# A fp32 decoder block on one core: the gate/up products of the FFN with the weight tiles stationary and h^T moving

## The chip, the cores and the metric

The kernel runs on one core of one Trainium2 chip. The metric is device time in microseconds (us) of one execution. Three runs of the kernel before took 446.09, 446.21 and 446.27 us; the median is 446.21 us.

## The reference, cut to what matters

A decoder block over 256 tokens of width 1024, all in float32: two branches (a causal convolution of 31 taps with layer norm, and attention over 8 heads), gated and merged, then a SwiGLU feed-forward with d_ff = 2816.

```python
n = rmsnorm(x, norm1_g);  z = n @ w_in                 # 1024 x 7168
cu, cg, q, k, v, gc, ga = split(z)
merged = sigmoid(gc) * conformer_conv(cu, cg) + sigmoid(ga) * (attention(q, k, v) @ w_attn_out)
h = x + merged @ w_out
h = h + (silu(r @ w_gate) * (r @ w_up)) @ w_down       # r = rmsnorm(h, norm2_g), d_ff = 2816
```

## The kernel before, in words

Every product is made of three products of float32r parts: the left operand is split in a high and a low part (h^T in `hh` and `hl`), the weights in `whi` and `wlo`, and high x high, low x high and high x low are summed in PSUM (`mm3`, lines 141 to 143).

The work is a list of 146 slots. A slot is one piece of weights: 512 KB, two k-tiles of 128 rows by 512 columns. In a slot TensorE does 12 matmuls: for each of 2 token tiles and 2 k-tiles the three products. The stationary operand is a 128x128 tile of the left side (tokens as columns), the moving operand 512 columns of weights, and the sum is 128 tokens x 512 columns. So each matmul loads its own stationary tile and then streams 512 columns. The slots of the gate/up product are `gu0` to `gu10` (44 slots; a chunk holds 256 gate columns and the same 256 up columns), those of the down product `dn0`, `dn1` (22 slots).

The order is written out by hand. `stream_dma` issues weights from SP 11 slots ahead into 5 buffers `raw`; `stream_split` has ScalarE make `whi` (line 123) and VectorE or GpSimd make `wlo` (line 124) 6 slots ahead. Other work hangs on the slots in four lists: `pre` (ahead of the slot's matmuls), `jobs` (between the two token tiles), `post` (after them) and `late`. All engines run their own instructions in the order in which they were written.

At the start, `stream_dma` puts on SP, in turn: piece 0 part 0, `xt` tile 0, piece 0 part 1, `xt` tile 1, `xt` tiles 2 and 3, piece 1, and so on (`between`, `load_x`, line 605). ScalarE scales and rounds x (`xgh`, line 617), squares it (lines 627, 630), GpSimd adds the squares (lines 631, 633), and `first_norm`, after slot 4, has TensorE sum them over partitions (`ss`, line 648). `WARM` = 8 matmuls of zeros keep TensorE busy from the start (line 161).

After the last slot of the out projection (`out_done`), h is transposed by TensorE (`htr`, line 513, one half of its 8 k-tiles per column block), split into `hh` and `hl` (lines 518, 519), and its row sums of squares give `rstd2` (lines 525 to 528). Since tokens lie on the partitions of the sums, `rstd2` is a per-partition scalar. For each chunk, `ffn_done` computes silu(gate) on ScalarE (line 546), multiplies on VectorE (line 548), has TensorE transpose the result (`ftr`, line 560: 4 transposes of 128x128), and splits it into `fh` and `fl` (lines 561, 562), the stationary side of the down product.

Where tiles lie: SBUF tiles follow each other in the order of their pools, each rounded up to 32 bytes a partition. `raw`, `whi`, `wlo` (4096 bytes each) and the pairs in `t8` (`xg`, `ao`, `y`, `m`, `h`; 8192 bytes each) all start at the same place modulo 512 bytes. `fh` and `fl` start behind the pool `sm`. Its tiles other than `bst` (192 bytes), `mv`, `lr`, `s2` (32 each), and `sq`, `m`, `nmx`, `den` (two of 32 each) are multiples of 512 bytes: 192 + 3 x 32 + 8 x 32 = 544, so `fh` and `fl` lie 32 bytes past the place of the weights modulo 512.

At the end the last three slots of the second half of the down product are done per token tile, the last one in two halves of 256 columns (`end`, 36 matmuls of 256 columns), and `store` adds the residual (line 571).

Of the kernel before, what the change touches and what calls it, by code (L numbers as in the profile page):

```python
# [27 lines left out]
EPS = 1e-6  # L28
BIG = 1e30
# [22 lines left out]
WARM = 8  # L52
# [3 lines left out]
class Chunk:  # L56
    """CW output columns of one product, for all tokens: nk k-tiles in pieces of G."""

    def __init__(self, name, w, lhs, nk, done):
        self.name, self.w, self.lhs, self.nk, self.done = name, w, lhs, nk, done  # L60
        self.acc = None


@with_exitstack
def hybrid_block(ctx: ExitStack, tc: tile.TileContext, x, xT, par, w_in, w_co, w_ao, w_o, w_gu, w_dn, out):
# [20 lines left out]
    def add(*chunks):  # L86
        """One chunk, or two of which each half is done in turn."""
        n = chunks[0].nk // G
# [7 lines left out]

    def parts(i):
        return [slice(j, j + 1) for j in range(G)] if i < 3 else [slice(0, G)]

    def stream_dma(upto):  # L100
        while at["dma"] < min(upto, len(slots)):
            i = at["dma"]
            c, g = slots[i]
            raw[i] = wp.tile([P, G, CW], F32, tag="raw", bufs=RAW_BUFS, name=f"raw{i}")
# [8 lines left out]
    def stream_split(upto):  # L113
        while at["split"] < min(upto, len(slots)):
            i = at["split"]
            hi[i] = wp.tile([P, G, CW], F32R, tag="whi", bufs=SPL_BUFS, name=f"whi{i}")
            lo[i] = wp.tile([P, G, CW], F32R, tag="wlo", bufs=SPL_BUFS, name=f"wlo{i}")
# [14 lines left out]

    def mm3(c, i, g, t, acc=None, cols=slice(0, CW), first=0, last=None):
        """Piece g of the chunk for token tile t; the sum runs from k-tile first to last."""
        xh, xl = c.lhs()
        acc = c.acc[t] if acc is None else acc
        last = c.nk - 1 if last is None else last
        tok = slice(t * P, (t + 1) * P)
        for j in range(G):
            k = g * G + j  # L140
            nc.tensor.matmul(acc, xh[:, k, tok], hi[i][:, j, cols], start=(k == first), stop=False)  # L141
            nc.tensor.matmul(acc, xl[:, k, tok], hi[i][:, j, cols], start=False, stop=False)  # L142
            nc.tensor.matmul(acc, xh[:, k, tok], lo[i][:, j, cols], start=False, stop=(k == last))  # L143

# [1 line left out]
    prm = cst.tile([P, N_PAR], F32, name="prm")  # L146
    xt = ea.tile([P, KD, S + 1], F32, tag="vs", name="xt")
    xs = cst.tile([P, T, D], F32, name="xs")

# [1 line left out]
    warm = cst.tile([P, CW], BF16, name="warm")  # L151
# [6 lines left out]
    load_table(AF.Sigmoid)  # L158
    wps = bank("wps", CW)
    for _ in range(WARM):  # L160
        nc.tensor.matmul(wps, warm[:, :P], warm, start=True, stop=True)
    ident = cst.tile([P, P], F32, name="ident")
    make_identity(nc, ident)
    mhalf = cst.tile([P, 8], F32, name="mhalf")
# [40 lines left out]
    def refill(ch):  # L205
        """The channels of the next tile go on the partitions, after KC - 1 zeros."""
# [17 lines left out]
    def run_taps(slot, until):  # L224
        while load["dve"] + TAP <= until:
# [94 lines left out]
    def normed(name, b):  # L320
        def done(slot, acc):
            st = {}

            def squares(t):
# [3 lines left out]
                for h in range(4):  # L328
                    junk = sm.tile([P, P], F32, tag="junk", name="junk")
# [37 lines left out]
    def head(first, slot, h):  # L367
# [15 lines left out]
        def score():  # L383
            s["bias"] = sm.tile([P, 3, P], F32, tag="bias", name=f"bias{h}")
            nc.scalar.mul(s["bias"], dist, 2.0 ** (-8.0 * (h + 1) / H))
            s["sc"] = bank(f"sc{h}", 4, P)
            nc.tensor.matmul(s["sc"][:, 0, :], s["q"][:, :P], s["k"][:, :P], start=True, stop=True)
            nc.tensor.matmul(s["sc"][:, 1:3, :], s["q"][:, P:], s["k"], start=True, stop=True)
# [106 lines left out]
    s2 = sm.tile([P, T, 2], F32, bufs=1, name="s2")  # L495

    def out_done(b):
        cols = slice(b * CW, (b + 1) * CW)

        def done(slot, acc):  # L500
# [4 lines left out]
            def turn():  # L505
                if not hT:
                    hT[0] = pair("h")
# [14 lines left out]
            def squares():  # L522
# [3 lines left out]
                if b:  # L526
# [9 lines left out]
    ff = {}  # L536

    def ffn_done(c):
        def done(slot, acc):
            f = {}  # L540

            def gate():
                for t in range(T):
                    r = rstd2[:, t : t + 1]
                    sg = sm.tile([P, 256], F32, tag="e0", name=f"fs{c}{t}")
                    nc.scalar.activation(sg, acc[t][:, :256], AF.Silu, scale=r)  # L546
                    f[t] = sm.tile([P, 256], F32, tag="e1", name=f"f{c}{t}")
                    nc.vector.scalar_tensor_tensor(f[t], acc[t][:, 256:], r, sg, op0=ALU.mult, op1=ALU.mult)  # L548

            def turn():  # L550
                if not ff:
                    early.close()
                    late_pool = ctx.enter_context(tc.tile_pool(name="ff", bufs=1))
                    ff[0] = (late_pool.tile([P, KF, S], F32R, name="fh"), late_pool.tile([P, KF, S], F32R, name="fl"))
                fh, fl = ff[0]
                k2 = slice(2 * c, 2 * c + 2)
                tr = bank(f"ftr{c}", 2, S)
                for j in range(2):
                    for t in range(T):
                        nc.tensor.transpose(tr[:, j, t * P : (t + 1) * P], f[t][:, j * P : (j + 1) * P], ident)  # L560
                nc.scalar.copy(fh[:, k2, :], tr)  # L561
                nc.vector.tensor_sub(fl[:, k2, :], tr, fh[:, k2, :].bitcast(F32))

            pre[slot + 1].append(gate)
            jobs[slot + 2].append(turn)
        return done
# [27 lines left out]
    ffn = [Chunk(f"gu{c}", w_gu[c], lambda: hT[0], KD, ffn_done(c)) for c in range(FF // 256)]  # L594
    add(*ffn[:2])
    for c in ffn[2:]:
        add(c)
# [4 lines left out]
    xg[0] = pair("xg")  # L602

    def load_x(k0, k1):
        nc.sync.dma_start(xt[:, k0:k1, :], xT[:, k0:k1, :])

    def between(i, part):
        if i == 0:
            load_x(part.start, part.stop)
# [5 lines left out]
    def split_x(k):  # L615
        g = xt[:, k, S:]
        nc.scalar.activation(xg[0][0][:, k, :], xt[:, k, :S], AF.Copy, scale=g)
        nc.vector.scalar_tensor_tensor(xg[0][1][:, k, :], xt[:, k, :S], g, xg[0][0][:, k, :].bitcast(F32),
                                       op0=ALU.mult, op1=ALU.subtract)

    stream_dma(AHEAD)
    sq = ea.tile([P, 2, S], F32, tag="yt", name="sq0")

    def square(q):
        """Squares of x, summed over the parts of its rows that share a partition."""
        if q == 0:
            nc.scalar.activation(sq, xt[:, :2, :S], AF.Square)
            return
        s = sm.tile([P, 2, S], F32, tag="u", name=f"xsq{q}")
        nc.scalar.activation(s, xt[:, 2 * q : 2 * q + 2, :S], AF.Square)  # L630
# [11 lines left out]
    ones = cst.tile([P, 1], F32, name="ones")  # L642
    nc.gpsimd.memset(ones, 1.0)

# [18 lines left out]
    for slot, (c, g) in enumerate(slots):  # L663
        for job in pre.pop(slot, ()):
            job()
        if g == 0:
            c.acc = [ps.tile([P, CW], F32, tag="mm", bufs=4, name=f"{c.name}_{t}") for t in range(T)]
        if slot < n - tail:
# [5 lines left out]
        if slot < n - tail:  # L674
            mm3(c, slot, g, 1, last=split_k - 1 if c is slots[-1][0] else None)
            if slot == n - tail - 1:
                nc.vector.tensor_add(xs[:, 1, D - CW :], xs[:, 1, D - CW :], c.acc[1])
# [17 lines left out]
        if g == c.nk // G - 1:  # L695
# [50 lines left out]
```

## Time and profile before

| | |
|---|---|
| time, median of 3 runs | 446.21 us (446.09 to 446.27) |
| span of the profiled execution | 443.5 us (its own time is not listed apart; the median less the span is 2.7 us) |
| TensorE matmuls (PE) | busy 437.6 us, 99% of the span, 2026 records |
| weight loads (PEld) | busy 359.6 us, 81% |
| VectorE (DVE) | 309.6 us, 70% |
| ScalarE (ACT) | 243.9 us, 55% |
| GpSimd (POOL) | 87.5 us, 20% |
| gate/up stage | 252.6 to 377.7 us of the span |

PE records are pipelined: a matmul of 512 columns shows 390 ns, but the next one starts some 230 ns after it. What counts is the distance between starts, called the pitch here. A product of plain float32 operands shows as two records. The weight load of a matmul stands in a row of its own (PEld) and overlaps the matmul ahead of it.

### The profile page before, as it was taken

The numbers are of one execution on the slowest core, as the hardware profiler recorded it, in microseconds if no ns is written. First come the engines' busy times: TensorE is split into PE (matmuls) and PEld (weight loads), VectorE is DVE, ScalarE is ACT, GpSimd is POOL, SyncE is SP. The second block draws the span as 40 slices with busy tenths as digits, with TensorE's granted clock in tenths as the row PEclk, the third lists the DMA queues.
The fourth block names the chain that finished last, engine by engine and source line by source line (L and its number), as shares of the span: only waits on it lengthen the run. The fifth ranks groups of instructions, "written<-read, shape, count | busy, mean of one in ns | idle before, by whom it ended". The sixth has DMA issues, their size and how long they took to land.

```text
span 443.5 us, 5743 instructions
## 1 busy us (share of the span) xinstructions
PE 437.6 (99%) x2026; PEld 359.6 (81%) x2026; DVE 309.6 (70%) x523; ACT 243.9 (55%) x439; POOL 87.5 (20%) x73
## 2 busy tenths in 40 slices
PE   8999999999999999999999999999999999999997
PEld 4788888888888888888888888888888888888886
DVE  5989999898899799967586575555555555644501
ACT  6854466689998676639325374444444444633200
POOL 1614465745462443100000000000000000000000
PEclk9999999999999999999999999999999999999999
DMA  8986684355345444544837337655555555585001
GB/s 274 345 271 213 211 303 150 144 185 197 142 149 185 142 137 150 190 163 161 293 95 247 133 120 253 196 189 184 184 185 179 187 181 184 184 252 204 25 0 49
DMA packets 23340, 80.21 MB, mean 181 GB/s; under 512 B 2576, under 2 KB 3216, under 8 KB 23312
## 3 DMA queue, kind: packets, MB, share of 16 engines
q1 hardware_dynamic: 22896, 78.66, 52.9%
q10 hardware_dynamic: 416, 1.19, 0.8%
q8 instruction: 16, 0.26, 0.3%
q14 instruction: 12, 0.10, 0.1%
HBM read 78.79 MB, written 1.05 MB: 180 GB/s over the span
## 4 chain that ended last, share of the span: by engine, by line
PE 94%; POOL 2%; ACT 2%; DMA 1%; SPq 0%; issue 0%; DVE 0%
PE gu L141 9%; PE gu L143 9%; PE gu L142 9%; PE dn L141 4%; PE dn L143 4%; PE dn L142 4%; PE g L143 3%; PE g L142 3%; PE g L141 3%; PE conv L141 2%; PE conv L143 2%; PE conv L142 2%; PE k L143 2%; PE v L143 2%; PE q L143 2%; PE q L141 2%
## 5 line engine op out<-in xcount | busy, mean ns | idle before, releaser
L124 DVE TENSOR_TENSOR wlo<-raw,whi 128x1024 fp32r<-128x1024 f32 (+1 forms) x125 | 153.0, 1256 | 30.5 <-ACT whi L123 29.6
L123 ACT CAST whi<-raw 128x1024 fp32r<-128x1024 f32 (+1 forms) x149 | 148.9, 1035 | 34.9 <-PE dn L142 19.8
L221 DVE SCALAR_TENSOR_TENSOR cacc<-cv,prm,cacc 128x256 f32<-128x256 f32 x240 | 97.2, 475 | 0.2
L141 PE MATMUL gu<-whi,hh 128*128 128x512 f32 x176 | 69.6, 395 | 0.0
L124 POOL TENSOR_TENSOR wlo<-raw,whi 128x1024 fp32r<-128x1024 f32 x24 | 58.1, 2426 | 54.5 <-ACT whi L123 49.6
L143 PE MATMUL gu<-wlo,hh 128*128 128x512 f32 x176 | 68.7, 390 | 0.0
L142 PE MATMUL gu<-whi,hl 128*128 128x512 f32 x176 | 68.5, 389 | 0.0
L143 PEld LDWEIGHTS gu<-wlo,hh 128*128 128x128 f32 x176 | 33.0, 188 | 7.1
L142 PEld LDWEIGHTS gu<-whi,hl 128*128 128x128 f32 x176 | 33.1, 188 | 6.6
L141 PEld LDWEIGHTS gu<-whi,hh 128*128 128x128 f32 x176 | 33.1, 188 | 6.4
L141 PE MATMUL dn<-whi,fh 128*128 128x512 f32 x82 | 32.5, 396 | 0.0
L143 PE MATMUL dn<-wlo,fh 128*128 128x512 f32 x82 | 32.4, 396 | 0.0
L142 PE MATMUL dn<-whi,fl 128*128 128x512 f32 x82 | 32.4, 396 | 0.0
L546 ACT ACTIVATE fs<-gu,rstd 128x256 f32<-128x256 f32 x22 | 10.4, 475 | 39.1 <-PE gu L143 39.1
L548 DVE SCALAR_TENSOR_TENSOR f<-gu,rstd,fs 128x256 f32<-128x256 f32 x22 | 10.6, 484 | 29.1 <-ACT fs L546 29.1
L141 PE MATMUL conv<-whi,xgh 128*128 128x512 f32 x64 | 26.1, 409 | 0.9 <-ACT whi L123 0.8
L141 PE MATMUL g<-whi,xgh 128*128 128x512 f32 x64 | 26.6, 415 | 0.0
L142 PE MATMUL conv<-whi,xgl 128*128 128x512 f32 x64 | 25.4, 398 | 0.0
L143 PE MATMUL conv<-wlo,xgh 128*128 128x512 f32 x64 | 25.4, 397 | 0.0
L143 PE MATMUL g<-wlo,xgh 128*128 128x512 f32 x64 | 25.2, 394 | 0.0
L142 PE MATMUL g<-whi,xgl 128*128 128x512 f32 x64 | 25.0, 391 | 0.0
L561 ACT CAST fh<-ftr 128x512 fp32r<-128x512 f32 x11 | 6.5, 587 | 23.9 <-PE ftr L560 23.9
(159 smaller groups left out, 746.4 us busy)
## 6 DMA issues: line engine op xcount, KB each, us to landing
raw<-in_w_in SPq DMA_DIRECT2D x53, 512.0 KB, 4.2
raw<-in_w_gu SPq DMA_DIRECT2D x44, 512.0 KB, 4.3
raw<-in_w_dn SPq DMA_DIRECT2D x22, 512.0 KB, 4.1
raw<-in_w_ao SPq DMA_DIRECT2D x8, 512.0 KB, 3.3
raw<-in_w_co SPq DMA_DIRECT2D x8, 512.0 KB, 3.3
raw<-in_w_o SPq DMA_DIRECT2D x8, 512.0 KB, 5.1
raw<-in_w_in SPq DMA_DIRECT2D x6, 256.0 KB, 4.7
xs<-in_x ACTq DMA_DIRECT2D x1, 1024.0 KB, 4.7
```

Source lines behind the costliest of these rows:

```text
L123: nc.scalar.copy(hi[i][:, part, :], r[:, part, :])
L124: eng.tensor_sub(lo[i][:, part, :], r[:, part, :], hi[i][:, part, :].bitcast(F32))
L141: nc.tensor.matmul(acc, xh[:, k, tok], hi[i][:, j, cols], start=(k == first), stop=False)
L142: nc.tensor.matmul(acc, xl[:, k, tok], hi[i][:, j, cols], start=False, stop=False)
L143: nc.tensor.matmul(acc, xh[:, k, tok], lo[i][:, j, cols], start=False, stop=(k == last))
L221: nc.vector.scalar_tensor_tensor(cacc[j], src, w, cacc[j], op0=ALU.mult, op1=ALU.add)
L546: nc.scalar.activation(sg, acc[t][:, :256], AF.Silu, scale=r)
L548: nc.vector.scalar_tensor_tensor(f[t], acc[t][:, 256:], r, sg, op0=ALU.mult, op1=ALU.mult)
L561: nc.scalar.copy(fh[:, k2, :], tr)
```

## The change: what it does

- Gate/up: the roles are swapped. A slot is still 512 KB, now `U` = 8 tiles of 128x128 weights. Each is stationary, h^T moves (256 tokens, 256 columns), and the sum is 128 columns of the FFN x 256 tokens. A slot has 24 matmuls of 256 columns (`mm_cols`). The sums use six banks in turn; the first six columns do k-tiles 0 to 3 of all six, then 4 to 7 (`halves_first`).
- The result is already transposed: the `ftr` transposes are gone. Gate and up of the same 128 columns follow each other; gate x rstd2 (DVE), silu (ACT), product with up (DVE), `fh` (ACT), `fl` (DVE), each on 128x256. `rstd2` now belongs to the free dimension: for the gate it is spread over the partitions by a product of ones with a diagonal matrix (`spread2` on DVE, `row2` on PE and ACT in the fifth slot of gate/up); for up it is left out and applied when the output is stored (`store`).
- Places: `h` is shifted by `SHIFT` = 48 words (192 bytes), the pairs get 512 bytes of room, `s2` takes 512 bytes, `junk` one buffer of 512 bytes fewer.
- Start: `xt` is one row of 16 + 2048 words, each x part is issued ahead of its weights, the first weights go out on ScalarE's queue, the table load stands behind it, `ones` is set early, `WARM` = 10.
- The convolution's `norm_back` steps 2 and 4 move from `post` to `jobs`; the two score products of a head change places.

```diff
-WARM = 8
+WARM = 10
+U = G * CW // P
+SHIFT = 48
+def halves_first(cols, nk, first):
+    half = nk // 2
+    out = [(c, k) for ks in (range(half), range(half, nk)) for c in range(first) for k in ks]
+    return out + [(c, k) for c in range(first, cols) for k in range(nk)]
+GU_BANKS = ("cv0", "cv1", "mm", "mm", "mm", "mm")
+GU_ORDER = halves_first(2 * KF, KD, len(GU_BANKS))
...
             for part in parts(i):
-                nc.sync.dma_start(raw[i][:, part, :], c.w[g][:, part, :])
+                if i == 0:
+                    load_x(part.start, part.stop)
+                (nc.sync if i or part.start else nc.scalar).dma_start(raw[i][:, part, :], c.w[g][:, part, :])
                 between(i, part)
...
-    def pair(name):
-        return (
-            t8.tile([P, KD, S], F32R, tag="t8h", name=name + "h"),
-            t8.tile([P, KD, S], F32R, tag="t8l", name=name + "l"),
+    def pair(name, shift=0):
+        return tuple(
+            t8.tile([P, KD * S + P], F32R, tag="t8" + x, name=name + x)[:, shift : shift + KD * S]
+            .rearrange("p (k s) -> p k s", s=S) for x in "hl"
...
+    def mm_cols(c, i, g, units, slot):
+        xh, xl = c.rhs()
+        for u in units:
+            n, k = c.order[g * U + u]
+            c.seen[n] += 1
+            first, last = c.seen[n] == 1, c.seen[n] == c.nk
+            if first:
+                tag = GU_BANKS[banks["n"] % len(GU_BANKS)]
+                banks["n"] += 1
+                c.acc[n] = ps.tile([P, S], F32, tag=tag, bufs=4 if tag == "mm" else 1, name=f"{c.name}{n}")
+            acc = c.acc[n]
+            nc.tensor.matmul(acc, hi[i][:, u, :], xh[:, k, :], start=first, stop=False)
+            nc.tensor.matmul(acc, hi[i][:, u, :], xl[:, k, :], start=False, stop=False)
+            nc.tensor.matmul(acc, lo[i][:, u, :], xh[:, k, :], start=False, stop=last)
+            if last:
+                c.done(slot, n, c.acc.pop(n))
...
-                            (post if i % 2 else jobs)[at_ + 2 + i // 2].append(lambda i=i: norm_back(2 * i))
+                            jobs[at_ + 2 + i // 2].append(lambda i=i: norm_back(2 * i))
...
-    s2 = sm.tile([P, T, 2], F32, bufs=1, name="s2")
+    s2 = sm.tile([P, 128], F32, bufs=1, name="s2")[:, : 2 * T].rearrange("p (t b) -> p t b", b=2)
...
-                    hT[0] = pair("h")
+                    hT[0] = pair("h", SHIFT)
...
                     rsqrt_mean(rstd2, rstd2, D, T)
+                    spread2()
+                    jobs[slot + 5].append(row2)
...
+    def spread2():
+        diag = second["diag"] = free("diag")
+        for t in range(T):
+            nc.vector.tensor_scalar_mul(diag[:, t * P : (t + 1) * P], ident, rstd2[:, t : t + 1])
+    def row2():
+        rb = bank("rb", S)
+        nc.tensor.matmul(rb, second["ones"], second["diag"], start=True, stop=True)
+        second["row"] = free("row2", "kT")
+        nc.scalar.copy(second["row"], rb)
+    def ffn_done(slot, n, acc):
+        j, up = divmod(n, 2)
...
+            nc.vector.tensor_mul(st["g"], acc, second["row"])           # scaled
+            nc.scalar.activation(st["s"], st["g"], AF.Silu)             # silu
+            nc.vector.tensor_mul(st["f"], acc, st["s"])                 # product
+            nc.scalar.copy(ff[0][0][:, j, :], st["f"])                  # high
+            nc.vector.tensor_sub(ff[0][1][:, j, :], st["f"], ff[0][0][:, j, :].bitcast(F32))  # low
+        if not up:
+            st["at"] = at_ = max(slot + 1, gu_slot + 5)
+            pre[at_].append(scaled)
+            late[at_].append(silu)
+        else:
+            at_ = max(slot + 1, st["at"] + 1)
+            pre[at_].append(product)
+            late[at_].append(high)
+            pre[at_ + 1].append(low)
...
-        nc.vector.tensor_add(o, acc, xs[:, t, to])
+        nc.vector.scalar_tensor_tensor(o, acc, rstd2[:, t : t + 1], xs[:, t, to], op0=ALU.mult, op1=ALU.add)
```

## Rows read from the trace of the kernel before

**Rows 1.** The page: busy times, and the chain that ended last by engine.

```profile
PE 437.6 (99%) x2026; PEld 359.6 (81%) x2026; DVE 309.6 (70%) x523; ACT 243.9 (55%) x439; POOL 87.5 (20%) x73
...
PE 94%; POOL 2%; ACT 2%; DMA 1%; SPq 0%; issue 0%; DVE 0%
```

**Rows 2.** Timeline, PE, gate/up between two transposes (start, duration, instruction).

```profile
303.65 0.40 PE L141 MATMUL gu<-whi,hh 128*128 128x512 f32 x1
...
313.64 0.39 PE L143 MATMUL gu<-wlo,hh 128*128 128x512 f32 x1
```

**Rows 3.** Timeline, PE, down product and its 256-column end.

```profile
424.83 0.40 PE L142 MATMUL dn<-whi,fl 128*128 128x512 f32 x1
...
435.57 0.40 PE L143 MATMUL dn<-wlo,fh 128*128 128x512 f32 x1
435.80 0.28 PE L141 MATMUL end<-whi,fh 128*128 128x256 f32 x1
...
439.94 0.28 PE L143 MATMUL end<-wlo,fh 128*128 128x256 f32 x1
```

**Rows 4.** Busy time of each engine in the gate/up stage.

```profile
252.60:377.70 125.10, 125.10 (x576) 103.63 (x575) 73.11 (x85) 62.28 (x89) 0.89 (x2) 1.00 0.58 183
```

**Rows 5.** Timeline, the start: warm-up, slow and fast matmuls, the first norm.

```profile
0.72 1.28 ACT L156 ACT_TABLE_LOAD   x1 [0.72 <-PEq L735]
...
1.18 3.60 PE L161 MATMUL wps<-warm 128*128 128x512 bf16 x8 [1.18 <-DVE warm L152]
...
5.59 0.80 PE L141 MATMUL conv<-whi,xgh 128*128 128x512 f32 x1 [0.82 <-ACT whi L123]
...
8.38 0.63 PE L143 MATMUL conv<-wlo,xgh 128*128 128x512 f32 x1
...
9.23 0.44 PE L142 MATMUL conv<-whi,xgl 128*128 128x512 f32 x1
...
22.01 0.52 PEld L648 LDWEIGHTS ss<-ones,sq 128*128 128x128 f32 x4 [0.95 <-POOL ones L643]
22.01 0.61 PE L648 MATMUL ss<-ones,sq 128*128 128x1 f32 x4 [0.53 <-POOL ones L643]
```

**Rows 6.** Timeline, around one group of transposes of the FFN.

```profile
302.53 0.60 PE L560 MATMUL ftr<-ident,f 128*128 128x128 f32 x4
302.88 0.47 PE L141 MATMUL gu<-whi,hh 128*128 128x512 f32 x1
...
303.20 0.39 PE L142 MATMUL gu<-whi,hl 128*128 128x512 f32 x1
```

**Rows 7.** The chain that ended last, in order of time: start, and gate/up.

```profile
2.10 4.17 DMA xt<-in_xT
6.29 0.51 ACT xgh L617
...
91.50 0.43 PE sc L388 x2
...
256.81 0.87 PE htr L513 x8
...
274.04 0.44 PE ftr L560 x4
```

**Rows 8.** Timeline, DVE and POOL, after the last half of h^T.

```profile
260.79 0.48 DVE L519 SCALAR_TENSOR_TENSOR hl<-htr,prm,hh 128x256 fp32r<-128x256 f32 x1 [0.54 <-ACT hh L518]
...
262.01 0.16 DVE L527 TENSOR_TENSOR rstd<-s 128x2 f32<-128x2 f32 x1 [0.74 <-ACT junk L525]
...
262.54 0.69 POOL L179 TENSOR_TENSOR rstd<-rstd,mhalf 128x2 f32<-128x2 f32 x1
262.95 1.22 DVE L124 TENSOR_TENSOR wlo<-raw,whi 128x1024 fp32r<-128x1024 f32 x1 [0.78 <-ACT whi L123]
```

**Rows 9.** Groups by line, ACT and DVE, 252 to 378 us (busy, mean ns).

```profile
L546 ACT ACTIVATE fs<-gu,rstd 128x256 f32<-128x256 f32 x21 | 10.0, 474 | 38.2 <-PE gu L143 38.2
L548 DVE SCALAR_TENSOR_TENSOR f<-gu,rstd,fs 128x256 f32<-128x256 f32 x21 | 10.2, 484 | 28.2 <-ACT fs L546 28.2
```

More of the change, by code (lines that the diff above doesn't have):

```diff
@@ L86, in add @@
     def add(*chunks):
+        if isinstance(chunks[0], Cols):
+            slots.extend((chunks[0], g) for g in range(len(chunks[0].order) // U))
+            return
         n = chunks[0].nk // G
@@ L95, in hybrid_block, with shape_of @@
     at = {"dma": 0, "split": 0}
+    def shape_of(i):
+        return (U, P) if isinstance(slots[i][0], Cols) else (G, CW)
     def parts(i):
-        return [slice(j, j + 1) for j in range(G)] if i < 3 else [slice(0, G)]
+        return [slice(j, j + 1) for j in range(G)] if i < 3 else [slice(None)]
     def stream_dma(upto):
@@ L115, in stream_split @@
             i = at["split"]
[L116 to L117 removed]
+            hi[i] = wp.tile([P, *shape_of(i)], F32R, tag="whi", bufs=SPL_BUFS, name=f"whi{i}")
+            lo[i] = wp.tile([P, *shape_of(i)], F32R, tag="wlo", bufs=SPL_BUFS, name=f"wlo{i}")
             r = raw.pop(i)
@@ L143, in mm3 @@
             nc.tensor.matmul(acc, xh[:, k, tok], lo[i][:, j, cols], start=False, stop=(k == last))
+    banks = {"n": 0}
+    def mm_cols(c, i, g, units, slot):
[14 more added lines that the diff above has]
+                c.done(slot, n, c.acc.pop(n))
     prm = cst.tile([P, N_PAR], F32, name="prm")
-    xt = ea.tile([P, KD, S + 1], F32, tag="vs", name="xt")
+    xt = ea.tile([P, XG + KD * S], F32, tag="vs", name="xt")
     xs = cst.tile([P, T, D], F32, name="xs")
-    warm = cst.tile([P, CW], BF16, name="warm")
+    warm = cst.tile([P, P], BF16, name="warm")
     nc.vector.memset(warm, 0.0)
@@ L156, in load_table @@
         nc.scalar.activation(tiny, warm[:, :1], func)
-    load_table(AF.Sigmoid)
-    wps = bank("wps", CW)
+    wps = bank("wps", 4, P)
     for _ in range(WARM):
-        nc.tensor.matmul(wps, warm[:, :P], warm, start=True, stop=True)
+        nc.tensor.matmul(wps, warm, warm[:, None, :].to_broadcast([P, 4, P]), start=True, stop=True)
     ident = cst.tile([P, P], F32, name="ident")
     make_identity(nc, ident)
+    ones = cst.tile([P, 1], F32, name="ones")
+    nc.gpsimd.memset(ones, 1.0)
     mhalf = cst.tile([P, 8], F32, name="mhalf")
@@ L328, in squares @@
                 for h in range(4):
-                    junk = sm.tile([P, P], F32, tag="junk", name="junk")
+                    junk = sm.tile([P, P], F32, tag="junk", bufs=1, name="junk")
                     nc.scalar.activation(junk, acc[t][:, h * P : (h + 1) * P], AF.Square, scale=r1(t),
@@ L386, in score @@
             s["sc"] = bank(f"sc{h}", 4, P)
+            nc.tensor.matmul(s["sc"][:, 1:3, :], s["q"][:, P:], s["k"], start=True, stop=True)
             nc.tensor.matmul(s["sc"][:, 0, :], s["q"][:, :P], s["k"][:, :P], start=True, stop=True)
-            nc.tensor.matmul(s["sc"][:, 1:3, :], s["q"][:, P:], s["k"], start=True, stop=True)
             most()
@@ L525, in squares @@
                     nc.scalar.activation(junk, xs[:, t, cols], AF.Square, accum_out=s2[:, t, b : b + 1])
-                if b:
+                if not b:
+                    second["ones"] = sm.tile([P, P], F32, tag="junk", bufs=1, name="allone")
+                    nc.gpsimd.memset(second["ones"], 1.0)
+                else:
                     nc.vector.tensor_add(rstd2, s2[:, :, 0], s2[:, :, 1])
                     rsqrt_mean(rstd2, rstd2, D, T)
+                    spread2()
+                    jobs[slot + 5].append(row2)
             pre[slot + 1].append(evac)
@@ L533, in out_done @@
         return done
[L536 to L566, printed above, removed]
@@ new lines, in hybrid_block, with free @@
+    ff, gates, second = {}, {}, {}
+    def free(name, tag="qT"):
+        return sm.tile([P, S], F32, tag=tag, bufs=4, name=name)
+    def spread2():
[7 more added lines that the diff above has]
+        nc.scalar.copy(second["row"], rb)
@@ L593, in hybrid_block @@
     add(*(Chunk(f"wo{b}", w_o[b], lambda: mT[0], KD, out_done(b)) for b in range(2)))
[L594 to L597, printed above, removed]
+    gu_slot = len(slots)
+    add(Cols("gu", w_gu, lambda: hT[0], KD, GU_ORDER, ffn_done))
     for b in range(2):
@@ L602, in hybrid_block, with xk @@
     xg[0] = pair("xg")
+    def xk(k0, k1):
+        return xt[:, XG + k0 * S : XG + k1 * S].rearrange("p (k s) -> p k s", s=S)
     def load_x(k0, k1):
-        nc.sync.dma_start(xt[:, k0:k1, :], xT[:, k0:k1, :])
+        cols = slice(XG + k0 * S if k0 else 0, XG + k1 * S)
+        nc.sync.dma_start(xt[:, cols], xT[:, cols])
     def between(i, part):
         if i == 0:
-            load_x(part.start, part.stop)
             if part.stop == G:
@@ L663, in hybrid_block @@
     for slot, (c, g) in enumerate(slots):
+        rows = isinstance(c, Chunk)
         for job in pre.pop(slot, ()):
             job()
-        if g == 0:
+        if not rows:
+            mm_cols(c, slot, g, range(U // 2), slot)
+        elif g == 0:
             c.acc = [ps.tile([P, CW], F32, tag="mm", bufs=4, name=f"{c.name}_{t}") for t in range(T)]
-        if slot < n - tail:
+        if rows and slot < n - tail:
             mm3(c, slot, g, 0)
@@ L673, in hybrid_block @@
             job()
-        if slot < n - tail:
+        if not rows:
+            mm_cols(c, slot, g, range(U // 2, U), slot)
+        elif slot < n - tail:
             mm3(c, slot, g, 1, last=split_k - 1 if c is slots[-1][0] else None)
             if slot == n - tail - 1:
-                nc.vector.tensor_add(xs[:, 1, D - CW :], xs[:, 1, D - CW :], c.acc[1])
+                end = xs[:, 1, D - CW :]
+                nc.vector.scalar_tensor_tensor(end, c.acc[1], rstd2[:, 1:2], end, op0=ALU.mult, op1=ALU.add)
             for job in post.pop(slot, ()):
@@ L694, in hybrid_block @@
         run_taps(slot, load["pe"] + LAG)
-        if g == c.nk // G - 1:
+        if rows and g == c.nk // G - 1:
             c.done(slot, c.acc)
@@ L708, in cols, with tiles @@
         return w.reshape(k // (G * P), G, P, n // CW, CW).transpose(3, 0, 2, 1, 4)
+    def tiles(w, order):
+        k, n = w.shape
+        w = w.reshape(k // P, P, n // P, P).transpose(2, 0, 1, 3)
+        return np.stack([w[c, j] for c, j in order]).reshape(-1, U, P, P).transpose(0, 2, 1, 3)
     def vec(v):
@@ L731 @@
         "w_o": cols(i["w_out"][0]),
-        "w_gu": cols(gu),
+        "w_gu": tiles(gu, GU_ORDER),
         "w_dn": cols(i["w_ffn_down"][0]),
```

39 lines of the change are left out of this document (29 added, 10 removed).

## The prediction

> **What bounds the kernel now.** I read the page first. TensorE is busy 99% of the span, no other engine over 70%, and 94% of the chain that ended last is TensorE [rows 1]. So the time is a count of TensorE instructions times the distance between their starts, plus what TensorE waits for at the two ends. What another engine saves is worth nothing while its buffers hold.
>
> Next the timeline of TensorE, for the pitch. In gate/up the two rows are 44 steps apart: 9.99 us / 44 = 227.0 ns for 512 columns [rows 2]. In the down product it is 46 steps: 10.74 / 46 = 233.5 ns; in the end, 35 steps with 256 columns each: 4.14 / 35 = 118.3 ns [rows 3]. The same instruction thus has two pitches. What differs is the place: in gate/up the stationary tile lies at the place of the weights modulo 512, in the down product 32 bytes past it (the sum of tiles above). [...]
>
> Four transposes of the FFN put the next gate/up matmul off by 0.35 us, and the one after that starts 0.32 us later where 0.227 is usual [rows 6]: 0.44 us in all, as the chain says too [rows 7].
>
> **The change part by part.** *Gate/up matmuls.* [...] The old stage, 252.6 to 377.7, is 125.1 us [rows 4]: 528 x 0.227 = 119.9, ten groups of transposes at 0.44 = 4.4, the second `htr` at 0.87 [rows 7]. The new one is 1056 x p + 0.87 + `row2`. `row2` is a plain fp32 product of 128x256, as the score product that takes 0.43 us in two records [rows 7].
>
> For p, the trace has no pair of streams 192 bytes apart, so I bound it. [...] The loads have a floor of their own: four matmuls of one column each have their loads in 0.52 us, the last of which lasts 0.19, so one follows another at (0.52 - 0.19) / 3 = 0.110 us [rows 5]; four transposes give (0.60 - 0.27) / 3 = 0.110 as well [rows 6], with 0.27 the length of one. From above: 118.3 ns, one load per 256 columns at 32 bytes past [rows 3]. Half of the 227 of the same place would be 113.5. I take p = 111 ns: the floor of the loads with little excess, because the two places that the trace shows differ in excess by half, so the place counts, and 110 is measured with nothing else in the way. That gives 117.2 + 0.9 + 0.4 = 118.5 us, **6.6 us less**; with 118.3 it is 126.2, 1.1 more than before; with 107 it is 114.3, 10.8 less.
>
> The eleventh group of transposes falls into the down product: **0.4 less**.
>
> [...]
>
> *Down product.* `s2` grows from 32 to 512 bytes and `junk` loses 512: what stood at 544 is 512, so `fh` and `fl` come to the place of the weights. If the pitch follows, 246 matmuls x 6.5 ns = 1.6 us, and 36 x 3 ns = 0.1 in the end: **1.7 less**. The bound on the other side is 0.
>
> *Start.* The chain goes from the transfer of `xt` tile 1, issued at 2.10, landed at 6.29, on to ScalarE, which splits x and squares it [rows 7], to GpSimd and to `ss` at 22.01, where TensorE waits 0.53 us [rows 5]. The transfer moves two places up on SP, about 0.9 us earlier, and 256 KB of weights no longer stand ahead of it on that queue; but the bytes that ScalarE needs next (part 1 of piece 0) stay where they were. Bounds 0 and 1.1; I take **0.6 less**. Ten warm-up matmuls at (3.60 - 0.63) / 7 = 0.42 us last until 1.18 + 4.2 = 5.4 us, just ahead of the first product (5.59) [rows 5]: they fill a gap, and if x comes sooner they hold the first product up by 0.3 at most; cover is the 0.53 us wait at `ss`. The table load, 1.28 us from 0.72 on [rows 5], now stands behind one transfer's issue on ScalarE; it is over before 3 us, and the first product that waits for ScalarE came at 5.59. Without that cover it would cost its 1.28.
>
> *Other moves.* Two `norm_back` groups join their neighbours: two interruptions of 0.09 us fewer, **0.2 less**. The order of the score products changes no count: 0. The last `store` is a scalar_tensor_tensor of 128x256, 0.48 us [rows 9], where an add of the same size stood: 0.1 more.
>
> *Waits that could be new.* h^T: k-tile 4 is needed after 72 matmuls of 0.111 and 0.87 us, at about 261.5, and the last `hl` at 262.5; `hl` ended at 261.27 [rows 8], and the `htr` come 0.2 sooner. Covered by about a microsecond. `rstd2`: ready on GpSimd at 263.2 [rows 8], two DVE operations of at most 0.48 us, 264.2; `row2` stands in the middle of the fifth slot, at 252.6 + 4.5 x 2.66 + 0.9 = 265.5. Cover 1.3 us; one slot sooner it would be late by 1.4. VectorE now sits 1.0 us behind GpSimd at `spread2`; queued there are the `wlo` of slots 6 ahead, 16 us before they are needed, and behind these the `raw` buffers that SP waits for. Nothing of it reaches TensorE.
>
> Six banks: a sum is read one or two slots after its end and its bank is needed six sums later. Engines: even if nothing were taken away, 66 operations of 0.48 us put VectorE from 73.1 to 105 us, and 44 of 0.47 ScalarE from 62.3 to 83 [rows 4, 9], under 118.
>
> *Sum.* -6.6 - 0.4 - 1.7 - 0.6 - 0.2 + 0.1 = -9.4 us. The profiled span is 443.5; the 2.7 us outside it I leave as they are: 446.2 - 9.4 = **436.8 us**.
>
> **The rivals.** *The place does nothing.* Then a load per 256 columns costs what the end shows, p = 118.3, and the down product keeps its 233.5: 446.2 - 9.4 + 7.7 + 1.7 = 446.2 us, no change. [...] Against: 227 and 233.5 for the same instruction [rows 2, 3]. Half way, if only the down product follows its place: 444.5.
>
> *The excess is paid per load* (the other side). [...] It decides from p = 111 + 9.4 / 1.056 = 119.9 ns. The same holds if TensorE can't be fed two instructions per 111 ns for 117 us on end: the trace shows 118 ns, but for 36 matmuls only. [...]
>
> *TensorE waits in the first slots of gate/up* for `row2` or the upper half of h^T. The margins are about 1 us; if both are missed by as much as they now hold, it costs some 2 us: 439. For it: at 260 us ScalarE and VectorE already wait on each other for h^T [rows 8].
>
> **How the numbers follow.** The forecast (p from 107 to 116, places count) gets 0.70; TensorE waiting 0.07; the place doing nothing 0.13, of which 0.09 for the half-way case and 0.04 for no change; per load 0.10. The likeliest is 436.8. With p = 107 and the most from the start it is 446.2 - 9.4 - 4.2 - 0.5, about 432; that corner I leave out and begin at 433.5, p = 108 with the start as taken. The upper end takes in p = 118.3 with the down product following: 444.6. Outside stay per load, no change and the corner, under 0.2. Within 0.2% (0.9 us) is about what a measurement of this kernel can't tell from no change. Faster: 0.70 + 0.07 + 0.09 = 0.86; same 0.05, with the lowest part of per load; slower 0.09.
>
> **What would show it.** Steps of 110 to 112 ns between gate/up matmuls, over a stage of about 118.5 us; 118 there means the place is without effect, over 120 the per-load cost. Down product: 227 for 233.5. `ss` at about 21.4 in place of 22.01. No idle TensorE ahead of the first matmul of `row2` and of k-tile 4. The prediction fails most likely by p: each ns is 1.06 us.

## The result and the profile after

The kernel after takes 440.95 us, median of four executions, beside 446.15 for the kernel before. (One of the four, of 621.51 us at a mean granted clock of 0.66, is left out of the ratio.) The ratio of the means is 0.9878, with the interval 0.9855 to 0.9901: 5.4 us less. The forecast was 436.8 us, 9.4 less; the range of 433.5 to 444.6 holds the time. The profiled execution took 441.83 us with a span of 440.0; the two others have a span of 438.2 and took 440.07 and 440.00. That difference has a likely cause of its own, below.

The page of after, busy times and the chain by engine:

```profile
PE 433.4 (98%) x2514; PEld 378.1 (86%) x2514; DVE 316.7 (72%) x558; ACT 247.8 (56%) x451; POOL 90.1 (20%) x74
...
PE 93%; ACT 2%; POOL 2%; DMA 1%; DVE 1%; SPq 0%; issue 0%
```

Against [rows 1] TensorE is still the bound, with more instructions in less time. So the pitch decides again. After, timeline of TensorE: gate/up before and behind `row2` (`rb`), the down product, its end, and the store.

```profile
260.22 0.28 PE L191 MATMUL gu<-hl,whi 128*128 128x256 f32 x1
...
268.46 0.28 PE L192 MATMUL gu<-hh,wlo 128*128 128x256 f32 x1
268.58 0.59 PE L607 MATMUL rb<-diag,allone 128*128 128x256 f32 x2
...
269.13 0.28 PE L191 MATMUL gu<-hl,whi 128*128 128x256 f32 x1
...
376.37 0.28 PE L192 MATMUL gu<-hh,wlo 128*128 128x256 f32 x1
376.48 0.39 PE L173 MATMUL dn<-whi,fh 128*128 128x512 f32 x1
...
432.25 0.28 PE L173 MATMUL end<-whi,fh 128*128 128x256 f32 x1
...
436.45 0.28 PE L175 MATMUL end<-wlo,fh 128*128 128x256 f32 x1
```

Ahead of `row2` there are 70 steps from 260.22 to 268.46: 117.7 ns each (117.8 in the longer streams of the experiments). Behind it, 946 steps from 269.13 to 376.37: 113.4 ns. The same instructions at the same addresses have two pitches, and the change from one to the other falls on `row2`. The down product takes 55.77 us for 246 steps, 226.7 ns where [rows 3] had 233.5; in the end, 35 steps take 4.20 us, 120.0 ns where [rows 3] had 118.3.

The stage starts worse than that. After, timeline of TensorE, first column of gate/up:

```profile
254.65 0.38 PE L191 MATMUL gu<-hl,whi 128*128 128x256 f32 x1
254.86 0.28 PE L192 MATMUL gu<-hh,wlo 128*128 128x256 f32 x1
...
255.10 0.32 PE L191 MATMUL gu<-hl,whi 128*128 128x256 f32 x1
255.25 0.28 PE L192 MATMUL gu<-hh,wlo 128*128 128x256 f32 x1
255.53 0.38 PE L190 MATMUL gu<-hh,whi 128*128 128x256 f32 x1
256.05 0.39 PE L191 MATMUL gu<-hl,whi 128*128 128x256 f32 x1
256.28 0.28 PE L192 MATMUL gu<-hh,wlo 128*128 128x256 f32 x1
```

Five steps are long (0.21, 0.15, 0.28, 0.52, 0.23 us); over 117.8 ns each that is 0.80 us. The chain that ended last says for what:

```profile
252.09 0.45 PE htr L565 x4
...
252.56 0.48 ACT hh L570
...
253.07 0.50 DVE hl L571
...
254.10 0.89 DVE hl L571 x2
...
255.01 0.48 ACT hh L570
...
255.52 0.49 DVE hl L571
...
256.05 0.39 PE gu L191
```

ScalarE and VectorE take turns over the lower half of h^T, 0.5 us a step, and TensorE's second, third and fourth k-tile of the first column come faster than that.

The start, from the same chain of after, and the row of `ss` in the timeline:

```profile
2.10 5.34 DMA xt<-in_xT
...
7.47 0.91 ACT xgh L698 x2
...
20.66 1.60 POOL sq L715
...
22.31 0.60 PE ss L727 x4
22.91 0.34 PE conv L173
...
23.49 0.41 PE conv L175
...
26.45 0.43 PE conv L173
```

```profile
22.31 0.60 PE L727 MATMUL ss<-ones,sq 128*128 128x1 f32 x4 [1.80 <-POOL sq L715]
```

In [rows 7] the chain went over a transfer that landed at 6.29; now it goes over a later `xt` transfer that lands at 7.44, and `ss` is at 22.31 where [rows 5] has 22.01. TensorE waits 1.80 us for it, not 0.53, and behind the wait its steps of 512 columns are 0.43 us long until 26.9. Busy time of TensorE in three stretches of after (stretch and length, busy time with its instructions, granted clock, DMA share, GB/s):

```profile
8.20:20.50 12.30, 12.30 (x55) 1.00 0.97 367
...
23.50:26.90 3.40, 3.40 (x9) 0.52 0.85 290
26.90:40.00 13.10, 13.10 (x61) 1.00 0.66 235
```

The granted clock reads 1.00 from 8.2 to 20.5 us; behind the wait it is 0.52. Nine matmuls stand where 3.4 us have room for 15 at 0.227: eight steps of 0.43 cost 1.6 us over 0.227.

By the starts of the first instruction of each stage in the two profiled executions:

| stretch | predicted | measured |
|---|---|---|
| start, to the first transpose into `cv` (29.39 to 31.30) | -0.6 | +1.9 |
| from there to gate/up (252.56 to 254.17) | -0.2 | -0.3 |
| gate/up (125.40 to 122.31) | -6.6 | -3.1 |
| down product (57.84 to 55.77) | -2.0 | -2.1 |
| end, 36 matmuls (4.14 to 4.20) | -0.1 | +0.06 |
| behind the last matmul (3.56 to 3.55) | +0.1 | 0.0 |
| sum | -9.4 | -3.5 |

The two other executions of after, 1.8 us shorter, have mean granted clocks of 0.999 and 1.000, the profiled one 0.996: by that they had no such fall, though no trace of them shows it. With it taken out the spans differ by 5.3 us (443.5 and 438.2). By the times they differ by more: 440.04 is 6.1 under the median before. Time and span lie 1.8 us apart in every execution of after, not the 2.7 that the table of the kernel before gives; by 1.8 the profiled execution before took some 445.3 us, an estimate, and was a short one.

### The profile page after: what moved, and what is told of

It reads as the page before. It is cut to its first block, busy times and chain, and to the rows that moved or that the text cites. A ratio compares the mean times of both kernels' runs of the same rounds, so it can differ in the third digit from the quotient of the medians.

```text
span 440.0 us, 6863 instructions
## 1 busy us (share of the span) xinstructions
PE 433.4 (98%) x2514; PEld 378.1 (86%) x2514; DVE 316.7 (72%) x558; ACT 247.8 (56%) x451; POOL 90.1 (20%) x74
## 4 chain that ended last, share of the span: by engine, by line
PE 93%; ACT 2%; POOL 2%; DMA 1%; DVE 1%; SPq 0%; issue 0%
PE gu L191 9%; PE gu L192 9%; PE gu L190 9%; PE dn L174 4%; PE dn L175 4%; PE dn L173 4%; PE g L175 3%; PE g L173 3%; PE g L174 3%; PE conv L173 2%; PE conv L175 2%; PE conv L174 2%; PE k L175 2%; PE k L173 2%; PE v L175 2%; PE q L173 2%
## 5 line engine op out<-in xcount | busy, mean ns | idle before, releaser
L190 PE MATMUL gu<-hh,whi 128*128 128x256 f32 x352 | 97.8, 278 | 0.0
L191 PE MATMUL gu<-hl,whi 128*128 128x256 f32 x352 | 97.6, 277 | 0.1
L192 PE MATMUL gu<-hh,wlo 128*128 128x256 f32 x352 | 97.4, 277 | 0.0
L155 POOL TENSOR_TENSOR wlo<-raw,whi 128x1024 fp32r<-128x1024 f32 x24 | 60.7, 2536 | 50.4 <-ACT whi L154 45.5
L191 PEld LDWEIGHTS gu<-hl,whi 128*128 128x128 f32 x352 | 66.1, 188 | 0.4 <-DVE hl L571 0.3
L190 PEld LDWEIGHTS gu<-hh,whi 128*128 128x128 f32 x352 | 66.1, 188 | 0.3 <-ACT hh L570 0.2
L192 PEld LDWEIGHTS gu<-hh,wlo 128*128 128x128 f32 x352 | 66.2, 188 | 0.0
L626 DVE TENSOR_TENSOR f<-gu,fs 128x256 f32<-128x256 f32 x22 | 9.2, 424 | 23.0 <-PE gu L192 23.0
L633 ACT CAST fh<-f 128x256 fp32r<-128x256 f32 x22 | 8.8, 406 | 26.8 <-DVE f L626 26.7
L622 ACT ACTIVATE fs<-fg 128x256 f32<-128x256 f32 x22 | 9.1, 417 | 25.4 <-DVE fg L618 25.4
```

What stands on the lines that cost most here:

```text
L190: nc.tensor.matmul(acc, hi[i][:, u, :], xh[:, k, :], start=first, stop=False)
L191: nc.tensor.matmul(acc, hi[i][:, u, :], xl[:, k, :], start=False, stop=False)
L192: nc.tensor.matmul(acc, lo[i][:, u, :], xh[:, k, :], start=False, stop=last)
L622: nc.scalar.activation(st["s"], st["g"], AF.Silu)
L626: nc.vector.tensor_mul(st["f"], acc, st["s"])
L633: nc.scalar.copy(ff[0][0][:, j, :], st["f"])
```

## The experiments

Ratios are to the kernel before, run on the same chip. All steps are TensorE's, worked out from the first and last start of a stretch without a break.

**1. h^T at the place of the weights** (p0).

```diff
-SHIFT = 48
+SHIFT = 0
```

> The changed kernel with SHIFT = 0: h^T at the place of the weights modulo 512, all else kept. Theory A, the place sets the excess and it is paid per load where both streams start at the same place: 14 ns on 107, as in the end of the changed kernel (256 columns, same place, steps of 120 ns): gate/up steps of about 120 ns where the changed kernel has 113.3, and 1056 x 6.7 = 7 us more than the changed kernel, so about 447, no faster than before. Theory B, the place does nothing for 256 columns and 113 is half of 227: gate/up steps of 113, the time of the changed kernel, about 441.

Measured: 447.92 us, 1.0034 (1.0019 to 1.0049). Timeline of this kernel, behind `row2` and at the end of gate/up:

```profile
268.98 0.28 PE L191 MATMUL gu<-hl,whi 128*128 128x256 f32 x1
...
382.49 0.28 PE L192 MATMUL gu<-hh,wlo 128*128 128x256 f32 x1
```

946 steps take 113.51 us: 120.0 ns, as in the end of after at the same place. So the place does it, and without it the change is slower than the kernel before, by 0.3%. At the place of the weights two matmuls of 256 columns take 240.0 ns where one of 512 takes 226.7 (down product of after): each one cut in two costs 13.3 ns more. That 256 columns alone take 107 ns, as the expectation has it, no trace shows; 226.7 - 120.0 = 106.7 ns is what 256 columns more cost at this place. Of ten executions seven had a mean clock of 0.996 and took 446.84 to 448.72 (median 448.06), three had 0.999 or 1.000 and took 446.35 to 446.61 (median 446.54). The profiled one, at 0.996, shows the fall behind a wait of 2.02 us for `ss` (steps of 0.43 us from 23.08 us on); that it costs this kernel some 1.5 us follows if the others fell there too.

**2. The old warm-up** (warm8).

```diff
-WARM = 10
+WARM = 8
```

> The changed kernel with 8 warm-up matmuls in place of 10, all else kept. Theory A, the ten keep TensorE busy until x comes, so its clock rises some 1.7 us sooner, TensorE reaches the first norm sooner and waits 1.8 us for GpSimd, and in some executions the clock falls back for 3.5 us (about 1.7 us lost): with 8 the wait at the first norm is some 0.5 to 1.2 us, no fall of the clock, ss again near 22.3, and the time is that of the changed kernel's better executions, about 440.0, in all executions. Theory B, the fall has nothing to do with the warm-up: the same spread of 440.0 to 441.8.

Measured: 441.23 us, 0.9891 (0.9852 to 0.9929). TensorE's steps are 0.23 us from 7.6 us on (after: 8.1); it waits 1.91 us for `ss`, and its clock falls behind that wait (mean granted clock of the profiled execution 0.995). The two further warm-up matmuls cause neither the early short steps nor the fall. Gate/up ran at 113.4 ns from the wait for h^T at its beginning on; after had the same wait and stayed at 117.8 until `row2`.

**3 and 4. A map of places** (pl_a, pl_b): all pairs moved, h^T's halves each to its own place; `FSHIFT` is the shift of `fh` and `fl` in words.

```diff
-SHIFT = 48
+SHIFT = (0, 16)      # pl_b: (32, 64)
+FSHIFT = 96          # pl_b: 24
...
-            yT[0] = pair("y")
+            yT[0] = pair("y", 32)       # pl_b: 8
-                aoT[0] = pair("ao")
+                aoT[0] = pair("ao", 16) # pl_b: 80
-                    mT[0] = pair("m")
+                    mT[0] = pair("m", 64)  # pl_b: 120
-    xg[0] = pair("xg")
+    xg[0] = pair("xg", 48)              # pl_b: 112
```

> The changed kernel with other places, one look for the steps between TensorE's starts. Bytes past the weights' place modulo 512: hh 0, hl 64, xg 192, ao 64, y 128, m 256, fh and fl 384. Theory A, the place sets the excess: gate/up steps after which h^T is read from the same place about 120 ns, those at 64 another value; of the products with 512 columns, steps other than 227 for at least two of conv/q/k/v/g (192), ao (64), co (128), wo (256), dn (384), between 213 and 240. Theory B, only 32 bytes past is odd: 227 in all of them, and gate/up as in the changed kernel, 113.

> As the look before with bytes past the weights' place modulo 512: hh 128, hl 256, xg 448, ao 320, y 32, m 480, fh and fl 96. Theory A, the place sets the excess: co (32 past) shows 233 as the down product of the kernel before did; the others differ from each other by 5 ns or more; gate/up differs between hh and hl. Theory B: 227 everywhere but co, gate/up 113.

Measured, one execution each: 447.46 and 450.94 us. Mean steps with 512 moving columns, by bytes of the activations past the weights, modulo 512:

| 0, 256 | 32, 64, 320, 480 | 96 | 128, 384 | 192, 448 |
|---|---|---|---|---|
| 227 | 233.4 | 234.2 | 232.4 | 228.9 |

Places 256 bytes apart agree (0 and 256, 64 and 320, 128 and 384, 192 and 448), and none beats 227. With 256 columns the order is another: 120.0 at 0, 118.3 at 32 [rows 3], 118.6 at 384, 117.4 at 96 (the last three from 36 matmuls each). Gate/up with halves at 0 and 64, timeline of `pl_a` ahead of and behind `row2`:

```profile
260.16 0.28 PE L193 MATMUL gu<-hl,whi 128*128 128x256 f32 x1
...
268.54 0.28 PE L194 MATMUL gu<-hh,wlo 128*128 128x256 f32 x1
...
269.21 0.28 PE L193 MATMUL gu<-hl,whi 128*128 128x256 f32 x1
...
380.63 0.28 PE L194 MATMUL gu<-hh,wlo 128*128 128x256 f32 x1
```

70 steps of 119.7 ns, then 946 of 117.8: here too the pitch changes at `row2`. Halves at 128 and 256 gave 120. Of the places tried only 192 past shows 113.4. The weights stayed where they were in all of this, so the runs don't tell the distance between the operands from the place of the activations as such.

**5. No wait for the lower half of h^T** (order): the first six columns go k-tile by k-tile, four columns and then two.

```diff
-    out = [(c, k) for ks in (range(half), range(half, nk)) for c in range(first) for k in ks]
+    out = [(c, k) for ks in (range(half), range(half, nk)) for cs in (range(4), range(4, first)) for k in ks for c in cs]
```

> The changed kernel with the first tiles of gate/up in another order: k-tile by k-tile over four columns (then over two), where the changed kernel does k-tiles 0 to 3 of one column first. Theory A, TensorE waits some 1.1 us in the first slot of gate/up because k-tiles 1 to 3 of h^T are not split yet when the first column asks for them: no step over 130 ns among the first twelve matmuls of gate/up, the stage 1.0 us shorter (121.3 for 122.3), the time 1 us under the changed kernel. Theory B, the wait only moves, to the upper half of h^T or to a bank of the out projection that is still being read: the stage stays 122.3.

Measured: 443.69 us, 0.9957 (0.9943 to 0.9972). The long steps are gone and the kernel is slower than after. Its timeline behind `row2` and at the end of gate/up:

```profile
266.82 0.28 PE L191 MATMUL gu<-hl,whi 128*128 128x256 f32 x1
...
378.24 0.28 PE L192 MATMUL gu<-hh,wlo 128*128 128x256 f32 x1
```

946 steps are 117.8 ns each: it never came to 113.4. Gate/up takes 125.7 us (252.67 to 378.36), as long as before. 947 x 4.4 ns less the 0.8 of the wait is 3.4 us, and the executions with a mean clock of 0.999 or more have 443.35 and 440.0 us. Neither theory had that: the wait costs 0.8 us, and without the added products of experiment 9 only kernels with after's order, which have the wait, came to the better pitch.

**6. The first norm a slot later** (later), with the first gate of the convolution.

```diff
-            first = slot + (2 if p == 0 else 1)
+            first = slot + (3 if p == 0 else 1)
...
-    post[4].append(first_norm)
+    post[5].append(first_norm)
```

> The changed kernel with the first norm one slot later (after slot 5 for slot 4) and the first convolution gate a slot later. Theory A, the 1.8 us that TensorE waits at the first norm, and the fall of its clock behind that wait in some executions, are what the start loses: the wait is gone, no matmul of 512 columns behind ss at 0.43 us, the first transposes of the convolution (cv) come at 29.5 to 30 for 31.3, and the time is 1.8 to 3.5 us under the changed kernel, about 437.5 to 439. Theory B, the convolution's chain on VectorE then comes late and something behind it waits by as much: 440 to 441.

Measured: 439.22 us (438.73 to 439.53), 0.9849 (0.9835 to 0.9862), the fastest kernel of this study: 1.7 us under after, where 1.8 to 3.5 was expected. Its timeline around `ss`, and its granted clock in the stretch that stands above for after:

```profile
22.62 0.39 PE L175 MATMUL conv<-wlo,xgh 128*128 128x512 f32 x1
22.85 0.50 PE L727 MATMUL ss<-ones,sq 128*128 128x1 f32 x4
23.21 0.48 PE L173 MATMUL conv<-whi,xgh 128*128 128x512 f32 x1
```

```profile
23.50:26.90 3.40, 3.40 (x16) 1.00 0.89 254
```

No wait, no fall: a granted clock of 1.00 for 0.52, 16 matmuls for 9. Against the two executions of after at 0.999 and 1.000 (440.04 us) the kernel is 0.8 us faster, against the profiled one (441.83) 2.6: most of that is the clock's. Gate/up ran at 113.4 ns from the wait for h^T on. All nine executions of the two kernels with this edit (this one and the next) have a mean clock of 0.999 or 1.000; of 22 without it (after, p0, warm8, order; the one of 621.51 us not counted) thirteen were at 0.996 or less. That speaks for the wait at `ss` as what lets the clock fall. But 0.996 is not a sign of this loss alone: of 24 executions of the kernel before beside these, thirteen have it too, and their median is only 0.1 to 0.5 us above that of the others. Where in the span their clock fell is not shown.

**7. Both edits** (both).

> Both edits on the changed kernel: the first tiles of gate/up k-tile by k-tile, and the first norm a slot later. Theory A: the two waits are independent and the gains add: 2.8 to 4.5 us under the changed kernel, about 437. Theory B, either wait only moves: 440 or more.

Measured: 443.02 us, 0.9936 (0.9923 to 0.9948). Its timeline at `row2` and at the end of gate/up:

```profile
265.24 0.60 PE L607 MATMUL rb<-diag,allone 128*128 128x256 f32 x2
...
265.79 0.28 PE L191 MATMUL gu<-hl,whi 128*128 128x256 f32 x1
...
377.20 0.28 PE L192 MATMUL gu<-hh,wlo 128*128 128x256 f32 x1
```

946 steps of 117.8 ns; `row2` does not help here, and the two gains don't add, though not for the reason of Theory B. Against the kernel of experiment 6 it is 3.8 us slower: 1056 x 4.4 ns is 4.6, less 0.8.

**8. The down product's place alone** (dn_place), in the kernel before.

```diff
-                    junk = sm.tile([P, P], F32, tag="junk", name="junk")
+                    junk = sm.tile([P, P], F32, tag="junk", bufs=1, name="junk")
...
-    s2 = sm.tile([P, T, 2], F32, bufs=1, name="s2")
+    s2 = sm.tile([P, 128], F32, bufs=1, name="s2")[:, : 2 * T].rearrange("p (t b) -> p t b", b=2)
```

> The kernel before with nothing changed but the places of fh and fl: s2 takes 512 bytes and junk one buffer fewer, so that they lie at the place of the weights modulo 512. Theory A, the place sets the excess of the down product: its steps 227 for 233.5, 1.6 us less, 444.4; the end with 256 columns is slower, 120 for 118.3. Theory B, the down product's 233.5 comes from something else: 446.

Measured: 444.11 us, 0.9963 (0.9950 to 0.9976). Timeline, behind the last `ftr` and near the end of the down product:

```profile
382.56 0.39 PE L142 MATMUL dn<-whi,fl 128*128 128x512 f32 x1
...
433.80 0.39 PE L143 MATMUL dn<-wlo,fh 128*128 128x512 f32 x1
```

226 steps of 226.7 ns for 233.5: the place alone makes the step. The end goes to 119.7 (after: 120.0). TensorE's steps were 0.23 us early here too (from 7.9 us on), with the old start, and it waited 1.81 us for `ss` without a fall behind it (steps of 0.23 us from 22.89 on, mean granted clock 1.000).

**9. Six breaks put into gate/up** (kick): the kernel of experiment 7 with six small plain float32 products, whose results nobody uses, six slots apart.

```diff
+    def kick(i, width):
+        kb = bank(f"kick{i}", 4, P)
+        nc.tensor.matmul(kb[:, 0, :width], ident, dist[:, 1, :width], start=True, stop=True)
+
+    for i, width in enumerate((1, 32, 64, 96, 128, 1)):
+        jobs[gu_slot + 8 + 6 * i].append(lambda i=i, width=width: kick(i, width))
```

> The kernel with both edits, whose gate/up runs at 117.8 ns from end to end, with six small plain products (ident with 1, 32, 64, 96, 128 and 1 columns of dist, into a bank that nobody reads) in the middle of the 9th, 15th, 21st, 27th, 33rd and 39th slot of gate/up. Theory A, at 192 bytes TensorE has two steady ways to go, 117.8 and 113.3 ns, and a break in its stream can throw it from one into the other: after at least one of the six the steps become 113.3 and stay so until a later one. Theory B, the order of the first 48 tiles itself makes 117.8 (places of the sums in the banks, buffers of the weights): 117.8 between all of them.

Measured, one execution: 442.46 us. Timeline of TensorE, the six products:

```profile
277.82 0.28 PE L679 MATMUL kick<-dist,ident 128*128 128x1 f32 x2
...
294.39 0.30 PE L679 MATMUL kick<-dist,ident 128*128 128x32 f32 x2
...
311.58 0.33 PE L679 MATMUL kick<-dist,ident 128*128 128x64 f32 x2
...
328.15 0.36 PE L679 MATMUL kick<-dist,ident 128*128 128x96 f32 x2
...
344.72 0.38 PE L679 MATMUL kick<-dist,ident 128*128 128x128 f32 x2
...
361.91 0.28 PE L679 MATMUL kick<-dist,ident 128*128 128x1 f32 x2
```

Between two of them lie 144 matmuls and some 0.25 us of the product itself. The distances are 16.57, 17.19, 16.57, 16.57 and 17.19 us: the pitch is 113.4, 117.8, 113.4, 113.4, 117.8, and 113.4 ns behind the last. Ahead of the first it is 117.8. A break can throw the stream from either pitch to the other, and between breaks neither drifts.

**10 and 11. The neighbours of the place** (both44, both52): the kernel of experiment 7 with h^T 176 and 208 bytes past.

```diff
-SHIFT = 48
+SHIFT = 44           # both52: 52
```

> The kernel with both edits and h^T 176 bytes past the weights' place, one look. Theory A, near 192 there is a place with one way to go alone, the fast one: 113 to 114 ns all through gate/up, the stage 121 for 125.7. Theory B, the two ways belong to the whole neighbourhood, and without a break ahead it stays in the slow one: 117 to 118.

> As the kernel before it, with h^T 208 bytes past the weights' place. Theory A: 113 to 114 ns all through gate/up. Theory B: 117 to 118.

Measured, one execution each: 444.10 and 443.90 us; 946 steps behind `row2` of 119.3 (265.80 to 378.62) and 119.2 ns (265.69 to 378.42). 192 is better than either side, by 1.4 ns even in its slower pitch. Gate/up takes 127.2 us in both, longer than the 125.4 of before.

**12. The six breaks at the place of the weights** (kick0): experiment 9 with `SHIFT = 0`.

> The kernel with the six small products in gate/up, with h^T at the place of the weights (SHIFT = 0), one look. Theory A, the place is what makes the fast way possible: 120 ns before and behind each of the six, no part of the stage at 113, about 447. Theory B, the fast way is there at any place and the kernel with SHIFT = 0 only never met a break that threw it there: 113 to 114 behind at least one of the six.

Measured, one execution: 447.18 us; 120 ns ahead of and behind every break. So the breaks alone don't make a second pitch: at the place of the weights there is none. The other places had no such breaks.

## Why the prediction was right in sign and too low by four microseconds

**The pitch p of gate/up was mis-sized.** By the spans, with the fall of the clock taken out, 4.1 us are missing of 9.4; gate/up has 3.5 of them and the start 0.7. The stage adds up: 1056 x 113.36 ns = 119.7, 109 matmuls in the slower pitch at 4.4 ns more = 0.5, the wait for h^T 0.8, the second `htr` 0.87, `row2` 0.44; together 122.3, as measured. The forecast of 118.5 had p = 111: 2.5 us too little. The 113.5 that stood among the bounds, half of 227, was the better value. The prediction took the floor of the loads, 110 ns, with little excess, for a place that no row of it showed; over that floor 3.4 ns stayed in the better pitch and 7.8 in the other. The 107 ns that its sum and its range take for 256 columns alone no row and no run shows, nor the excess over it that its choice of p names: what the runs showed is that 256 columns more cost 106.7 ns at the place of the weights (226.7 - 120.0, after) and 115.2 ns 32 bytes past (233.5 - 118.3, [rows 3]), and no pitch with 256 columns under 113.4. What the doubled loads cost goes with the place: two matmuls of 256 columns take 240.0 ns for one of 226.7 at the place of the weights, 236.6 for 233.5 32 bytes past. Without the shift the time is 447.92 us with a p of 120.0, just over the 119.9 from which the per-load rival decides. The shift takes 6.6 ns off the 120.0, or 2.2 in the slower pitch. That gate/up gains at all hangs on the place and on the better pitch: in the slower one it takes 125.7 us (experiment 5), at both neighbours tried 127.2, and before 125.4.

**That the time lies in the range owes something to luck.** The prediction has one pitch; that there are two it did not foresee. Had gate/up kept behind `row2` the pitch that it had ahead of it, as the kernels of experiments 5 and 7 did, 947 x 4.4 ns = 4.2 us would have come on top: some 445.1 us, above the range.

**A step was missed: the lower half of h^T.** The prediction checked k-tile 4 and the last `hl` (both in time) but not k-tiles 1 to 3. Before, a slot was two k-tiles with 12 matmuls of 227 ns, so k-tile 2 was asked for 2.7 us into the stage; now a column runs through four k-tiles in 1.4 us. Cost 0.8 us. Experiment 5 showed that the repair is not free of consequences.

**The start was mis-sized, in sign too.** The transfer of tile 1 came sooner, and the one behind it became the chain; `ss` stayed between 21.95 and 22.39 us in the profiled executions of all eight kernels that keep `first_norm` behind slot 4. TensorE came sooner and so waited longer (0.53 to 1.80), and where the clock fell behind the wait it cost 1.6 to 1.8 us. Experiment 6 takes the wait away and with it the fall of the clock (1.00 granted from 23.5 to 26.9 us for 0.52). Why the steps come down to 0.23 us early, also with the old start in experiment 8, is not settled; the warm-up is not it (experiment 2).

**Right.** The down product: 226.7 ns and no `ftr`, -2.1 for -2.0, and experiment 8 gives the place alone. The stretch with the `norm_back` groups and the score products: -0.3 for -0.2. `row2` was not waited for: `diag` was ready at 265.8, the product stands at 268.58, a cover of 2.8 us. The last store is 0.48 us as taken. In the end the sign was wrong, by 0.16 us: with 256 columns the weights' place is the worse one (120.0 for 118.3).

**What stays open.** What the two pitches at 192 bytes are, and which breaks change them: the same wait for h^T led to 113.4 ns in two kernels and left after at 117.8. Whether one small product early in the kernel of experiment 7 would keep its pitch at 113.4 (some 4 us for 0.25) was not tried. Why the clock falls behind a wait of 1.8 to 2.0 us for `ss` in some executions only isn't settled either.

## What to carry to other kernels

Where every matmul loads its own stationary tile, halving the columns doubles the loads, and what that costs hung on the place here (13.3 ns for each matmul cut in two at the place of the weights, 3.1 ns 32 bytes past): measure the pitch at the place where both operands will lie before building on it, and watch for breaks that change it: 192 bytes past took 2.2 or 6.6 ns off 120 here, 176 and 208 bytes only some 0.8. When operands change roles, list again when each tile of them is first asked for, from the first k-tile on. Work that made TensorE reach `ss` sooner only lengthened its wait there (0.53 us before, 1.80 in after), and where the clock fell behind the wait, that cost another 1.6 us.

## What the runs showed of the hardware that was not expected

- One instruction stream at one place has two steady pitches, 113.4 and 117.8 ns, and a break of some 0.25 us can throw it from one to the other (experiment 9), as `row2` did in after (0.44 us). With halves at 0 and 64 the pitch changed at `row2` as well, from 119.7 to 117.8 (experiment 3); at the place of the weights there is one, 120.0 (experiment 12).
- The pitch depends on where the activations lie past the weights: 227 to 234 ns with 512 columns, alike at places 256 bytes apart, and 113.4 to 120.0 with 256 columns. The best place is not the same for both: 0 and 256 bytes past with 512 columns, 192 bytes past with 256 columns (experiments 1, 3, 4, 10, 11).
- Behind a wait of 1.80 us for `ss` in after TensorE's granted clock fell (0.52 from 23.5 to 26.9 us, steps of 0.43 us, at a cost of 1.6 us), and behind 2.02 and 1.91 us in experiments 1 and 2 (mean granted clock of the execution 0.996 and 0.995); behind waits of like length in experiments 3 (1.98 us, mean 0.999) and 8 (1.81 us, mean 1.000) it did not.
- The granted clock does not show every slow stretch at the start. Busy time of TensorE in the kernel before, columns as above:

```profile
8.20:9.50 1.30, 1.30 (x4) 1.00 1.02 382
```

Four matmuls of 512 columns stand there, with the steps of 0.425 us of [rows 5], and the clock reads 1.00; after has eight in the same stretch. So the pitch, not the clock's row, is what to read there.
